# A hybrid decoder block on one core: VectorE instead of GpSimd at the passage, B's second value projection traced ahead of a norm, and the bonus of B's second segment traced later

## The chip, the cores and the metric

The kernel runs on one NeuronCore of a Trainium2 chip. The metric is device time in microseconds (us) of one execution; the kernel before has a median of 2935.78 us over 3 runs (2934.64 to 2939.5 us). The engines are called as the profile calls them: PE is TensorE (matrix products), PEld its loading of weights, DVE is VectorE, ACT is ScalarE, POOL is GpSimd, SP is SyncE, which issues most of the DMAs.

## The reference

One decoder layer over 1024 tokens and 16 meta tokens ahead of them, 1024 channels wide, in float32:

```
h = h + 0.5 * swiglu(rmsnorm(h), ffn1_w_gu, ffn1_w_down)
u = rmsnorm(h, mix_norm)
aq, ak, av, az, abeta, aalpha, bcols, ga, gb = split(u @ w_in)
o_a = deltanet(aq, ak, av, az, abeta, aalpha, ...)   # 8 heads, chunks of 64
o_b = rwkv7(bcols, ...)                              # 16 heads of 64
h = h + (sigmoid(ga) * o_a + sigmoid(gb) * o_b) @ w_out
h = h + 0.5 * swiglu(rmsnorm(h), ffn2_w_gu, ffn2_w_down)
out = rmsnorm(h, final_norm)[:, 16:]
```

Inside the RWKV-7 branch (B in the code) three projections r, k and v of `u` are shifted (each token is mixed with the token before it), a state is carried through the sequence, and a bonus is added to its output:

```
zf = zf + (prev - zf) * mu            # the shift
r, k, v, wd, ad, gd = split(zf)
k = k * (1 + (a - 1) * k_a)
y = scan(state, r, decay, k, v, -kk, kk * a);  y = groupnorm(y)
y = y + sum(r * k * r_k, over a head) * v     # the bonus
```

The DeltaNet branch (A) runs short causal convolutions over its q, k and v, normalises q and k, and inverts a unit lower triangular matrix for every chunk of 64 tokens.

## The kernel before, in words

**Precision.** A product of float32 matrices is made as three products of rounded parts: every operand is held as a high part and a low part (`split`, lines 162 and 163: ACT writes the high part, another engine subtracts it from the source and writes the low part), and `mm3` adds high*high, high*low and low*high. So one projection tile of 128 output channels is 8 x 3 = 24 products over the 8 blocks of 128 input channels (the name `pp` in the profile, line 314).

**Stages.** The first feed-forward layer (`down` and its forms are the tail of it, products `pd`, line 741) runs to about 691 us. Then comes the *passage*: the mix norm turns the residual `h` into the operand `u`. The tokens are in two segments of 512 (the first with the 16 meta tokens, 528 columns). The norm of the first segment is made there: ACT squares the blocks (`nsq`, line 327), an adder sums them (line 334), PE adds over partitions (`nps`), DVE multiplies each block `h` by gain and 1/rms (`nt`, line 918), and `u_tile` splits the result (`uk`, lines 162 and 163). For the other segment only the sums of squares are made here; the norm itself is made later. In the kernel before, POOL adds those sums (7 adds) and makes three of the eight low parts `uk` (blocks 1, 3 and 5). Then the middle: 16 steps, 8 for each segment, each of which handles 128 channels of A and of B; then the output projection; then the second feed-forward layer from about 2260 us to the end.

**A step.** The middle is a list of actions traced in the order of the strings `FIRST`, `REGULAR` and so on; a `+` stands for the next step. `new_b` makes B's projections v (48), k (40) and r (32), each by `shifted`: PE projects, ACT and DVE (lines 1205 and 1206) shift. It ends with the bonus: `bv = r*rk*k` on DVE (line 1485), split into `hl` (lines 162 and 163), two products `bon` with a block of ones (line 1292) and a multiplication by v on DVE (line 1490). `new_a` makes A's k, q and v with their convolutions (`acc`, line 1513) and column sums for the norms (`cs`, line 1292). `inverses` runs a long chain of small DVE instructions (`tb`, `Xb`, lines 1703 and 1705), copies the result (`Yt`, line 1706) and sends it through memory to `Xc`; `merge_blocks` (products `iv`, lines 1743 to 1767) joins the inverted blocks on PE with copies by ACT and DVE between: `Y` (line 1757), `XA` (line 1758), `T`. `operands` makes the products `grb` and `gra` and their masks (`LT`, line 1554). `norm` is the first action that deals with the segment that comes second.

**What sets the order.** Instructions are written by the trace, and a list scheduler of the framework then sets each engine's order from the order of tracing and its own estimate of when operands are ready; every engine takes its queue strictly in that order. `tc.issue_after` pins an instruction behind another. The number of buffers of a pool bounds how far ahead the scheduler can put work: projections write to PSUM tiles `mm` (two in the first segment, three in the second), column sums and the bonus to tiles `mx` (two, then three), and the parts `hl` have a single buffer, so that each user of `hl` waits for the products of the one before it.

Of the kernel before, what the change touches and what calls it, by code (L numbers as in the profile page):

```python
# [25 lines left out]
FULL = 512  # L26
# [131 lines left out]
def split(g, src, hi, lo, eng=None, hi_eng=None):  # L158
    if hi_eng:
        hi_eng.tensor_copy(hi, src)  # L160
    else:
        g.nc.scalar.activation(hi, src, AF.Copy)  # L162
    (eng or g.nc.vector).tensor_tensor(lo, src, hi.bitcast(F32), op=ALU.subtract)  # L163


LORA = (56, 57, 58)
USES = {"segment": LORA, "new_b": (48, 40, 32), "new_a": (8, 0, 16), "gates": (24, 59, 67)}


def schedule():  # L170
# [12 lines left out]

FIRST = "decay new_b tokens new_a decay+ operands norm inverses new_b+ new_a+"
REGULAR = "merge_blocks transitions operands+ inverses+ chains gates finish decay++ new_b++ finish_a new_a++"
BEFORE_SWITCH = "merge_blocks transitions operands+ inverses+ chains gates finish finish_a banks gates+ segment decay++ new_b++ tokens++ new_a++"
SWITCH = "merge_blocks transitions operands+ inverses+ chains finish decay++ new_b++ finish_a new_a++"
LAST_BUT_ONE = "merge_blocks transitions operands+ inverses+ chains gates finish finish_a"  # L190
FINAL = "gates merge_blocks transitions chains finish finish_a fill"

# [115 lines left out]
def mm3(g, ps, w, kk, rhs):  # L308
    n = 3 * kk
    i = 0  # L310
    for k in range(kk):
        hi, lo = rhs(k)
        for l, r in ((w[:, 0, k, :], hi), (w[:, 0, k, :], lo), (w[:, 1, k, :], hi)):
            g.last_product = g.nc.tensor.matmul(ps, lhsT=l, rhs=r, start=i == 0, stop=i == n - 1)  # L314
            i += 1


# [497 lines left out]
def ffn1(g):  # L815
    tc, nc = g.tc, g.nc
    n = T // 2
    with ExitStack() as ctx:
# [54 lines left out]
        def before_last():  # L873
# [5 lines left out]
            for x in ("t3", "22"):  # L879
# [9 lines left out]
            hidden.load(len(hidden.slots), LAST)  # L889
            logs(g)  # L890
            hooks.rms = [Rms(g, lambda: g.un.tile([P, 528], F32, name="nsq", tag="nsq", bufs=4), n,
                             add_on=nc.gpsimd if s else None) for s, (_, n, _) in enumerate(SEGS)]
            hooks.todo = []
            for s in range(2):
                for k in range(HK, KD):
# [2 lines left out]
        def squares(s, k):  # L898
            t0, sn, _ = SEGS[s]
            hooks.rms[s].add(hs[k][:, t0 : t0 + sn])  # L900
            nc.sync.dma_start(g.hdr[s][k], hs[k][:, t0 : t0 + sn])

        def after(r, m, s):
            if r < LAST:
                if r == LAST - 1 and m == HK - 1:
                    before_last()
                return
            squares(s, m)
            if m == HK - 1 and s == 0:
                rs = g.un.tile([P, 528], F32, name="nrs", tag="nrs", bufs=1)  # L910
                hooks.rms[s].finish(rs)
                g.u = []
                hooks.todo = [(k, rs) for k in range(KD)]
            elif m == HK - 1:
                nc.gpsimd.dma_start(g.rdr, hooks.rms[s].acc[:, :FULL])
            for k, rs in hooks.todo[: 2 * s]:
                t = hooks.nt[:, k]
                nc.vector.scalar_tensor_tensor(t, hs[k][:, SEGS[0][0] :], g.V("gm", k), rs, op0=ALU.mult, op1=ALU.mult)
                g.u.append(u_tile(g, t, nc.gpsimd if k in (1, 3, 5) else None))
            del hooks.todo[: 2 * s]  # L920

        hooks.after = after
        down(g, hs, 1, n, hidden, hooks)
# [208 lines left out]
def ch3(ap, c):  # L1132
    return ap.rearrange("p (a b) -> p a b", b=c)
# [161 lines left out]
def parts_tile(g, n):  # L1295

    t = g.st.tile([P, 2, 528], F32R, name="hl", tag="hl")
    return t[:, 0, :n], t[:, 1, :n]
# [137 lines left out]
    return q  # L1436


def new_b(g, q):

    nc, st, V, c, j, n, off, it = g.nc, g.st, g.V, q.c, q.j, q.n, q.off, q.it
# [2 lines left out]
    tmp = lambda name, w=528: tmp_tile(g, name, w)  # L1444
    EN, ELx, av, elm = q.EN, q.ELx, q.av, meta and q.elm

    v = shifted(g, c, 48 + j, 16 + j, "vB")


    Vs = q.Vs = st.tile([P, NCB, CB], F32, name="Vs", tag="Vs", bufs=2)  # L1450
# [32 lines left out]
    nc.vector.tensor_tensor(AR[:, NCB + 1 :], ch3(r[:, fs], CB), ELx[:, :, 1:], op=ALU.mult)  # L1483
    bv = q.bv = st.tile([P, FULL], F32, name="bv", tag="bv", bufs=2)
    nc.vector.scalar_tensor_tensor(bv, r[:, fs], V("rk", j), k[:, fs], op0=ALU.mult, op1=ALU.mult)
    ps = g.mx.tile([P, 512], F32, name="bon", tag="mx")
    hi, lo = parts_tile(g, FULL)
    split(g, bv, hi, lo)
    colsum(g, ps, "bd", hi, lo)
    nc.vector.tensor_tensor(bv, ps, v[:, fs], op=ALU.mult)  # L1490


def new_a(g, q):
# [233 lines left out]
def merge_blocks(g, q):  # L1727
# [28 lines left out]
    nc.scalar.activation(Y[0:32, :, 32:64], ch3(ps2[0:32, 0:384], 32), AF.Copy)
    nc.vector.tensor_copy(Y[64:96, :, 96:128], ch3(ps2[64:96, 0:384], 32))
    nc.vector.tensor_copy(XA[32:64, :, 0, :, :], ps2[32:64, 0 : NCA * 32].rearrange("p (t c r) -> p t r c", r=2, c=16))
# [215 lines left out]
def finish_a(g, q):  # L1974
# [11 lines left out]
    else:  # L1986
        g.last = yb


ACTIONS = {"new_b": new_b, "tokens": tokens, "new_a": new_a, "norm": norm, "operands": operands, "inverses": inverses, "merge_blocks": merge_blocks, "transitions": transitions,  # L1990
           "chains": chains,
           "gates": gates, "finish": finish, "finish_a": finish_a, "fill": fill}

# [85 lines left out]
```

## Time and profile before

| what | value |
|---|---|
| median of 3 runs | 2935.78 us (2934.64 to 2939.5) |
| the profiled execution, its own time | 2937.92 us |
| its span, first to last instruction | 2935.9 us |
| its mean granted PE clock | 0.993 |
| PE busy, of the span | 2829.0 us (96%) |
| DVE busy | 2198.7 us (75%) |
| ACT busy | 1445.4 us (49%) |
| POOL busy | 386.7 us (13%) |

PE is the engine with next to no room: all that the kernel can win without fewer products lies in the some 107 us in which PE is not busy, and in what the clock takes from it. So the profile is read by the places at which PE stands still: what released it there, and what the engine that released it had been doing. An entry such as `[1.09 <-ACT hl L162]` in a timeline says that PE had been idle for 1.09 us when an ACT instruction of line 162, which writes `hl`, let it go on.

### The profile page before, as it was taken

To read this page: it belongs to the slowest core of one execution; us is meant where nothing else is said; L and a number is where in the kernel's file an instruction comes from. 1 tells how busy PE (TensorE), PEld (TensorE's weight loads), DVE (VectorE), ACT (ScalarE), POOL (GpSimd) and SP (SyncE) were. 2 spreads that over 40 slices of the span, in tenths; PEclk is the share of its full clock that TensorE was granted. 3 is DMA by queue.
4 is the path that set the end of the run, shared out by engine and by line. 5 is a ranking of instruction groups with operands and counts; after the bars stand their busy time and mean duration, and the time that the engine had idled before them with its cause. 6 is when DMAs were issued, how large, how long until landed. Compare 5 with 4: busy or idle time off the path is not lost. (4 is left out here: it accounts for less than half of the span.)

```text
span 2935.9 us, 60624 instructions
## 1 busy us (share of the span) xinstructions
PE 2829.0 (96%) x24552; PEld 2447.1 (83%) x24552; DVE 2198.7 (75%) x4183; ACT 1445.4 (49%) x2511; POOL 386.7 (13%) x566
## 2 busy tenths in 40 slices
PE   8999999999899999999998999999999999999998
PEld 8999999999878887888776777777777888888887
DVE  8666567776678877788777888888877766667876
ACT  6322224346555656566566656656644422223443
POOL 0332320003000000000000110101101032232000
PEclk9999999999999999999999999999999999999999
DMA  5333226553232322333232332333355333223763
GB/s 215 127 109 103 101 99 226 189 193 126 67 78 73 88 65 76 78 82 94 82 99 67 94 77 73 80 87 85 112 142 184 129 108 104 101 95 129 259 213 112
DMA packets 287895, 339.16 MB, mean 116 GB/s; under 512 B 172704, under 2 KB 181024, under 8 KB 287616
## 3 DMA queue, kind: packets, MB, share of 16 engines
q1 hardware_dynamic: 283600, 326.10, 35.7%
q0 software_dynamic: 2000, 6.56, 0.6%
q8 instruction: 193, 3.16, 0.4%
q10 hardware_dynamic: 2016, 2.63, 0.3%
q14 instruction: 86, 0.70, 0.1%
HBM read 267.57 MB, written 73.41 MB: 116 GB/s over the span
## 5 line engine op out<-in xcount | busy, mean ns | idle before, releaser
L314 PE MATMUL pp<-uk,w 128*128 128x512 f32 (+2 forms) x4824 | 972.6, 347 | 7.4 <-ACT w L162 2.2
L314 PEld LDWEIGHTS pp<-uk,w 128*128 128x128 f32 x4824 | 745.3, 191 | 101.3 <-issue 5.6
L741 PE MATMUL pd<-form,w 128*128 128x256 f32 (+2 forms) x2904 | 435.1, 312 | 0.0
L741 PEld LDWEIGHTS pd<-form,w 128*128 128x128 f32 x2904 | 402.5, 189 | 32.3 <-issue 1.0
L520 PE MATMUL pg<-bt,w 128*128 128x256 f32 (+2 forms) x2520 | 401.6, 317 | 2.3 <-DVE w L163 2.3
L520 PEld LDWEIGHTS pg<-bt,w 128*128 128x128 f32 x2520 | 360.2, 188 | 36.3 <-DVE w L163 3.6
L526 DVE TENSOR_TENSOR c<-c,pg 128x520 f32<-128x520 f32 (+1 forms) x280 | 189.4, 688 | 247.4 <-PE pg L520 222.2
L163 DVE TENSOR_TENSOR w<-wraw,w 128x1024 fp32r<-128x1024 f32 (+1 forms) x254 | 334.1, 1316 | 41.9 <-ACT w L162 38.6
L520 PE MATMUL pg<-b,w 128*128 128x256 f32 (+2 forms) x2160 | 348.1, 317 | 1.1 <-DVE w L163 1.1
L162 ACT ACTIVATE w<-wraw 128x1024 fp32r<-128x1024 f32 (+1 forms) x254 | 267.0, 1052 | 161.1 <-PE pg L520 117.3
L520 PEld LDWEIGHTS pg<-b,w 128*128 128x128 f32 x2160 | 309.9, 188 | 29.4 <-DVE w L163 1.3
L162 ACT ACTIVATE w<-wrx 128x1024 fp32r<-128x1024 f32 (+1 forms) x64 | 58.4, 912 | 274.7 <-PE pg L520 246.2
L162 ACT ACTIVATE w<-wsum 128x768 fp32r<-128x768 f32 x96 | 75.7, 789 | 142.0 <-PE pd L741 116.7
L162 ACT ACTIVATE form<-form 128x520 fp32r<-128x520 f32 (+1 forms) x152 | 94.2, 632 | 83.6 <-DMA form<-frm 79.7
L1705 DVE TENSOR_TENSOR Xb<-Xb,tb 115x126 f32<-115x126 f32 (+22 forms) x496 | 125.6, 253 | 10.6
L490 POOL TENSOR_TENSOR wrx<-wrx 128x512 f32<-128x512 f32 x38 | 52.4, 1380 | 613.5 <-DVE w22b L163 440.6
L1703 DVE TENSOR_TENSOR tb<-Ub,Xb 115x126 f32<-115x126 f32 (+22 forms) x496 | 124.6, 251 | 9.1
L163 DVE TENSOR_TENSOR w<-wsum,w 128x768 fp32r<-128x768 f32 x96 | 87.2, 908 | 37.3 <-ACT w L162 37.2
L163 DVE TENSOR_TENSOR form<-form 128x520 fp32r<-128x520 f32 (+1 forms) x152 | 100.9, 697 | 17.6 <-ACT form L162 17.3
L1513 DVE SCALAR_TENSOR_TENSOR acc<-xr,pk,acc 128x528 f32<-128x528 f32 (+1 forms) x144 | 107.3, 756 | 5.9 <-ACT acc L1509 4.7
L314 PE MATMUL pwo<-uk,w 128*128 128x512 f32 x384 | 94.9, 397 | 2.1 <-DVE ho L1180 1.5
L314 PEld LDWEIGHTS pwo<-uk,w 128*128 128x128 f32 x384 | 70.2, 188 | 17.6 <-ACT w L162 2.8
(445 smaller groups left out, 4259.4 us busy)
## 6 DMA issues: line engine op xcount, KB each, us to landing
wraw<-in_win SPq DMA_DIRECT2D x150, 512.0 KB
wraw<-in_wgu SPq DMA_DIRECT2D x44, 512.0 KB
wrx<-in_wgu SPq DMA_DIRECT2D x44, 512.0 KB
frm<-c SPq DMA_DIRECT2D x76, 260.0 KB
form<-frm SPq DMA_DIRECT2D x76, 260.0 KB
frm<-c SPq DMA_DIRECT2D x76, 256.0 KB
form<-frm SPq DMA_DIRECT2D x76, 256.0 KB
wraw<-in_wdn SPq DMA_DIRECT2D x34, 384.0 KB
```

The source lines that it names most:

```text
L162: g.nc.scalar.activation(hi, src, AF.Copy)
L163: (eng or g.nc.vector).tensor_tensor(lo, src, hi.bitcast(F32), op=ALU.subtract)
L314: g.last_product = g.nc.tensor.matmul(ps, lhsT=l, rhs=r, start=i == 0, stop=i == n - 1)
L490: sums.tensor_tensor(a22, a21, a22, op=ALU.add)
L520: nc.tensor.matmul(ps[:, c0 : c0 + cn], lhsT=l[:, x, k, :], rhs=r[:, k, y, c0 : c0 + cn], start=i == 0, stop=i == 3 * HK - 1)
L526: nc.vector.tensor_tensor(o, x, y, op=ALU.add)
L741: nc.tensor.matmul(pd[:, c0 : c0 + cn], lhsT=wd[:, u, k - k0, :], rhs=x[:, v, c0 : c0 + cn], start=k + i == 0, stop=k == HF - 1 and i == 2)
L1513: nc.vector.scalar_tensor_tensor(acc[:, :n], xr[:, tap : tap + n], V("convw", ct * 4 + tap), acc[:, :n], op0=ALU.mult, op1=ALU.add)
L1703: nc.vector.tensor_tensor(tv, U[:, i, i + 1 :].unsqueeze(2).to_broadcast([npt, nt, ncc]), X[:, i, 0:ncc].unsqueeze(1).to_broadcast([npt, n ...
L1705: nc.vector.tensor_tensor(X[:, i + 1 :, 0:ncc], X[:, i + 1 :, 0:ncc], tv, op=ALU.add)
```

## The change

Four edits. (1) At the passage the adder of the second segment's sums and the low parts of blocks 1, 3 and 5 are DVE's instead of POOL's; for that segment the two norm multiplications and their splits are traced ahead of the square and add of the block just finished, where they stood behind them. The DMA `rdr` that stores the sums stays on POOL's queue. (2) `new_b` is cut: its value projection becomes an action of its own, `values_b`, traced right before `new_b` everywhere but in the opening, where the second step's `values_b` is traced ahead of `norm`. (3) The end of `new_b` becomes a function `bonus`; for the first segment it is called where it stood (with its PSUM tile taken after the split), for the second segment it is called in `new_a` after the second projection there, its products pinned behind the twelfth product of that projection. (4) In `merge_blocks` the copy `XA` is traced before the copy `Y` on DVE.

```
@@ schedule
-USES = {"segment": LORA, "new_b": (48, 40, 32), "new_a": (8, 0, 16), ...}
+USES = {"segment": LORA, "values_b": (48,), "new_b": (40, 32), "new_a": (8, 0, 16), ...}
-FIRST = "decay new_b tokens new_a decay+ operands norm inverses new_b+ new_a+"
-REGULAR = "... decay++ new_b++ finish_a new_a++"
+FIRST = "decay values_b new_b tokens new_a decay+ operands values_b+ norm inverses new_b+ new_a+"
+REGULAR = "... decay++ values_b++ new_b++ finish_a new_a++"
@@ mm3
+    g.products = []
...
+            g.products.append(g.last_product)
@@ the passage
-                             add_on=nc.gpsimd if s else None) for s, (_, n, _) in enumerate(SEGS)]
+                             add_on=None) for s, (_, n, _) in enumerate(SEGS)]
-            squares(s, m)
+            if not s:
+                squares(s, m)
...
-            elif m == HK - 1:
-                nc.gpsimd.dma_start(g.rdr, hooks.rms[s].acc[:, :FULL])
             for k, rs in hooks.todo[: 2 * s]:
...
-                g.u.append(u_tile(g, t, nc.gpsimd if k in (1, 3, 5) else None))
+                g.u.append(u_tile(g, t))
             del hooks.todo[: 2 * s]
+            if s:
+                squares(s, m)
+                if m == HK - 1:
+                    nc.gpsimd.dma_start(g.rdr, hooks.rms[s].acc[:, :FULL])
@@ new_b, bonus, new_a
+def values_b(g, q):
+    q.v_all = shifted(g, q.c, 48 + q.j, 16 + q.j, "vB")
...
-    v = shifted(g, c, 48 + j, 16 + j, "vB")
+    v = q.v_all
...
+    q.v = v[:, fs]
+    if meta:
+        bonus(g, q)
+def bonus(g, q, behind=None):
+    hi, lo = parts_tile(g, FULL)
+    split(g, q.bv, hi, lo)
     ps = g.mx.tile([P, 512], F32, name="bon", tag="mx")
-    hi, lo = parts_tile(g, FULL)
-    split(g, bv, hi, lo)
-    colsum(g, ps, "bd", hi, lo)
-    nc.vector.tensor_tensor(bv, ps, v[:, fs], op=ALU.mult)
+    with ExitStack() as queue:
+        if behind is not None:
+            queue.enter_context(g.tc.issue_after(behind.ins))
+        colsum(g, ps, "bd", hi, lo)
+    g.nc.vector.tensor_tensor(q.bv, ps, q.v, op=ALU.mult)
...
         ps = proj(g, c, ct)
+        if wi == 1 and not meta:
+            bonus(g, q, g.products[3 * HK - 1])
@@ merge_blocks
+    nc.vector.tensor_copy(XA[32:64, :, 0, :, :], ps2[32:64, 0 : NCA * 32].rearrange(...))
     nc.vector.tensor_copy(Y[64:96, :, 96:128], ch3(ps2[64:96, 0:384], 32))
-    nc.vector.tensor_copy(XA[32:64, :, 0, :, :], ps2[32:64, 0 : NCA * 32].rearrange(...))
```

How the order moves is read at three places. The first is DVE's queue at the passage, from the third of the last four blocks `h` on. Before:

```order
L918 SCALAR_TENSOR_TENSOR nt<-h_5076,pk,nrs 128x528
L918 SCALAR_TENSOR_TENSOR nt<-h_5074,pk,nrs 128x528
L918 SCALAR_TENSOR_TENSOR nt<-h_5081,pk,nrs 128x528
L163 TENSOR_TENSOR uk<-nt,uk 128x528 [waits Activation_49]
L918 SCALAR_TENSOR_TENSOR nt<-h_5078,pk,nrs 128x528
L163 TENSOR_TENSOR uk<-nt,uk 128x528 [waits Activation_49]
L748 SCALAR_TENSOR_TENSOR h_5076<-pd,h_5076 128x256 [waits PE_49]
L918 SCALAR_TENSOR_TENSOR nt<-h_5077,pk,nrs 128x528
L918 SCALAR_TENSOR_TENSOR nt<-h_5075,pk,nrs 128x528
L163 TENSOR_TENSOR uk<-nt,uk 128x528 [waits Activation_49] x2
L748 SCALAR_TENSOR_TENSOR h_5074<-pd,h_5074 128x256 [waits PE_49]
```

and with the change (line numbers are one or two higher there):

```order
L163 TENSOR_TENSOR uk<-nt,uk 128x528 [waits Activation_49] x2
L750 SCALAR_TENSOR_TENSOR h_5076<-pd,h_5076 128x256 [waits PE_49]
L919 SCALAR_TENSOR_TENSOR nt<-h_5081,pk,nrs 128x528
L919 SCALAR_TENSOR_TENSOR nt<-h_5078,pk,nrs 128x528
L336 TENSOR_TENSOR nsq<-nsq 128x512 [waits Activation_49]
L163 TENSOR_TENSOR uk<-nt,uk 128x528 [waits Activation_49] x2
L750 SCALAR_TENSOR_TENSOR h_5074<-pd,h_5074 128x256 [waits PE_49]
L919 SCALAR_TENSOR_TENSOR nt<-h_5077,pk,nrs 128x528
L919 SCALAR_TENSOR_TENSOR nt<-h_5075,pk,nrs 128x528
L336 TENSOR_TENSOR nsq<-nsq 128x512 [waits Activation_49]
L163 TENSOR_TENSOR uk<-nt,uk 128x528 [waits Activation_49] x2
```

All eight low parts and the adds are in DVE's queue now, in groups of one block `h`, two norms, one add and two low parts; the last two norms and low parts stand behind the last block of `h`, which waits for PE's last `pd` product.

The second place is PE's queue in the opening, where the first step's operands of A are made (`gm`, `bkt`, `vp`, `btp`, `ktp`, `vmp`) up to the first product `vbp` of the second step, which needs the shifted value projection `vB`. Before:

```order
L1600 MATMUL gm<-c3m,ck 16x16 [waits DVE_49,PE_49]
L1609 MATMUL gm_8579<-kq 16x16 [waits DVE_49,PE_49]
L1388 MATMUL bkt<-ck,BK 128x64 [waits DVE_49]
...
L1356 MATMUL vp<-LT,Vs 64x64 [waits Activation_49]
L1356 MATMUL vp<-LT,Vs 64x64 x15
L1356 MATMUL vp<-Vs,BKt 64x64 x5
L1641 MATMUL btp<-ck,bkm 64x128 [waits Activation_49]
L1646 MATMUL ktp<-ck,kq 128x128 [waits Activation_49]
L1646 MATMUL ktp<-ck,kq 128x128 x3
L1651 MATMUL vmp<-ck,kq 128x128 [waits Activation_49]
L351 MATMUL nps<-usq,ones 128x512 [waits DMAHW4_49,Activation_49]
L1356 MATMUL vbp<-ck,vB 64x64 [waits DVE_49]
```

and with the change:

```order
L315 MATMUL pp<-uk,w 128x272 x7
L1622 MATMUL gm<-c3m,ck 16x16 [waits DVE_49,PE_49]
L315 MATMUL pp<-uk,w 128x272 x8
L1631 MATMUL gm_8579<-kq 16x16 [waits DVE_49,PE_49]
L315 MATMUL pp<-uk,w 128x272 x7
L1393 MATMUL bkt<-ck,BK 128x64 [waits DVE_49]
...
L315 MATMUL pp<-uk,w 128x256 x9
...
L315 MATMUL pp<-uk,w 128x256 x6
L1361 MATMUL vp<-LT,Vs 64x64 [waits Activation_49]
L1361 MATMUL vp<-LT,Vs 64x64 x15
```

Between the waiting small products stand 47 products of the second step's r projection, in pieces; four stood there before. Its PSUM tile is free earlier because DVE's shift of `vB` is now ahead of the masks of `gra`.

The third place is PE's queue in a step of the second segment, from the products of q on (24 `pp` each make one projection). Before:

```order
L314 MATMUL pp<-uk,w 128x512 x24
L314 MATMUL pp<-uk,w 128x512 [waits Activation_49]
L314 MATMUL pp<-uk,w 128x512
L314 MATMUL pp<-uk,w 128x512 [waits DVE_49]
L314 MATMUL pp<-uk,w 128x512 x10
L1292 MATMUL bon<-hl,bdr 128x512 [waits PE_49,Activation_49]
L314 MATMUL pp<-uk,w 128x512 x7
```

and with the change, in the same step:

```order
L1297 MATMUL cs<-hl,onesr 128x512 [waits PE_49,Activation_49]
L1361 MATMUL vp<-Vs,BKt 64x64
L315 MATMUL pp<-uk,w 128x512 x2
L1297 MATMUL cs<-hl,onesr 128x512 [waits DVE_49]
L315 MATMUL pp<-uk,w 128x512 x8
L1297 MATMUL bon<-hl,bdr 128x512 [waits PE_49,Activation_49]
L315 MATMUL pp<-uk,w 128x512 x2
L1297 MATMUL bon<-hl,bdr 128x512 [waits DVE_49]
```

The two products `bon` stand behind A's k with its column sums instead of behind the first half of k's projection: some 80 products of 512 columns after the column sum of `kkn`, where it was 37.

More of the change, by code (lines that the diff above doesn't have):

```diff
@@ L166 @@
 LORA = (56, 57, 58)
-USES = {"segment": LORA, "new_b": (48, 40, 32), "new_a": (8, 0, 16), "gates": (24, 59, 67)}
+USES = {"segment": LORA, "values_b": (48,), "new_b": (40, 32), "new_a": (8, 0, 16), "gates": (24, 59, 67)}
 def schedule():
@@ L182, in schedule @@
                 yield act.rstrip("+"), it + act.count("+")
-FIRST = "decay new_b tokens new_a decay+ operands norm inverses new_b+ new_a+"
-REGULAR = "merge_blocks transitions operands+ inverses+ chains gates finish decay++ new_b++ finish_a new_a++"
-BEFORE_SWITCH = "merge_blocks transitions operands+ inverses+ chains gates finish finish_a banks gates+ segment decay++ new_b++ tokens++ new_a++"
-SWITCH = "merge_blocks transitions operands+ inverses+ chains finish decay++ new_b++ finish_a new_a++"
+FIRST = "decay values_b new_b tokens new_a decay+ operands values_b+ norm inverses new_b+ new_a+"
+REGULAR = "merge_blocks transitions operands+ inverses+ chains gates finish decay++ values_b++ new_b++ finish_a new_a++"
+BEFORE_SWITCH = "merge_blocks transitions operands+ inverses+ chains gates finish finish_a banks gates+ segment decay++ values_b++ new_b++ tokens++ new_a++"
+SWITCH = "merge_blocks transitions operands+ inverses+ chains finish decay++ values_b++ new_b++ finish_a new_a++"
 LAST_BUT_ONE = "merge_blocks transitions operands+ inverses+ chains gates finish finish_a"
@@ L1756, in merge_blocks @@
     nc.scalar.activation(Y[0:32, :, 32:64], ch3(ps2[0:32, 0:384], 32), AF.Copy)
+    nc.vector.tensor_copy(XA[32:64, :, 0, :, :], ps2[32:64, 0 : NCA * 32].rearrange("p (t c r) -> p t r c", r=2, c=16))
     nc.vector.tensor_copy(Y[64:96, :, 96:128], ch3(ps2[64:96, 0:384], 32))
-    nc.vector.tensor_copy(XA[32:64, :, 0, :, :], ps2[32:64, 0 : NCA * 32].rearrange("p (t c r) -> p t r c", r=2, c=16))
     ps3 = g.ch.tile([P, 512], F32, name="iv3", tag="ch")
@@ L1987, in finish_a @@
         g.last = yb
-ACTIONS = {"new_b": new_b, "tokens": tokens, "new_a": new_a, "norm": norm, "operands": operands, "inverses": inverses, "merge_blocks": merge_blocks, "transitions": transitions,
+ACTIONS = {"values_b": values_b, "new_b": new_b, "tokens": tokens, "new_a": new_a, "norm": norm, "operands": operands, "inverses": inverses, "merge_blocks": merge_blocks, "transitions": transitions,
            "chains": chains,
```

## Prediction

> **What bounds the kernel now.** I read the page first, for the engine without room.
>
> ```profile
> span 2935.9 us, 60624 instructions
> PE 2829.0 (96%) x24552; PEld 2447.1 (83%) x24552; DVE 2198.7 (75%) x4183; ACT 1445.4 (49%) x2511; POOL 386.7 (13%) x566
> ```
>
> PE is busy 96% of the span and the change adds no product, so a gain can only come out of the 2935.9 - 2829.0 = 107 us in which PE stands still, or out of products that run slower than they might. Next, the stretches that the change touches, side by side (busy time of each engine, then the granted PE clock).
>
> ```profile
> core 0: us, PE busy (x) PEld busy (x) DVE busy (x) ACT busy (x) POOL busy (x), PEclk, DMA share, GB/s
> 660.00:700.00 40.00, 37.23 (x287) 35.93 (x286) 30.76 (x36) 21.00 (x33) 16.92 (x12) 0.96 0.44 156
> 772.00:796.00 24.00, 17.73 (x253) 12.90 (x252) 13.79 (x37) 14.48 (x35) 1.55 (x7) 0.86 0.27 76
> 796.00:850.00 54.00, 49.19 (x382) 43.39 (x383) 42.78 (x106) 30.13 (x52) 6.83 (x16) 0.91 0.28 69
> 1600.00:2160.00 560.00, 533.38 (x5860) 416.05 (x5861) 464.15 (x1092) 339.25 (x639) 52.69 (x113) 1.00 0.32 86
> ```
>
> The passage (660 to 700) has 2.8 us of PE idle time, the opening (772 to 796) 6.3, the second segment (1600 to 2160) 26.6 in 560, that is some 4 in each step of 85 us. The opening and the passage also have a clock below 1. Stretches of 3.41 us show where it falls:
>
> ```profile
> 693.72:697.13 3.41, 1.25 (x5) 0.83 (x6) 3.32 (x4) 1.48 (x3) 3.14 (x3) 1.00 0.16 62
> 697.13:700.54 3.41, 3.40 (x16) 3.07 (x15) 0.88 (x3) 0.63 (x1) 1.81 (x2) 0.50 0.34 115
> 1577.77:1581.18 3.41, 1.11 (x4) 0.30 (x2) 3.41 (x9) 3.36 (x6) 3.21 (x6) 1.00 0.00 0
> 1581.18:1591.42 10.24, 8.34 (x45) 5.38 (x46) 9.65 (x24) 5.29 (x11) 0.43 (x1) 0.50 0.16 53
> 1840.60:1844.01 3.41, 2.81 (x12) 2.24 (x13) 3.41 (x5) 0.95 (x2) 3.03 (x4) 1.00 0.89 201
> ```
>
> In each pair a stretch in which PE was busy for 1.1 to 1.3 us of 3.41 is followed by one at half clock; 2.81 us of work (the stretch with the bonus' wait) is not punished. So a wait at the passage, in the opening or at the switch of segments costs its length and, where PE then has work, up to 1.7 us more for each half-clock stretch.
>
> **The passage.** DVE's queue and PE's waits there:
>
> ```profile
> 689.26 1.83 DVE L163 TENSOR_TENSOR uk<-nt,uk 128x528 fp32r<-128x528 f32 x1
> 691.01 0.76 DVE L918 SCALAR_TENSOR_TENSOR nt<-h,pk,nrs 128x528 f32<-128x528 f32 x1
> 691.69 0.69 DVE L163 TENSOR_TENSOR uk<-nt,uk 128x528 fp32r<-128x528 f32 x1
> 692.52 1.31 POOL L163 TENSOR_TENSOR uk<-nt,uk 128x528 fp32r<-128x528 f32 x1 [2.01 <-ACT uk L162]
> 692.64 3.46 DVE L918 SCALAR_TENSOR_TENSOR nt<-h,pk,nrs 128x528 f32<-128x528 f32 x2
> 693.89 0.51 PE L314 MATMUL pp<-uk,w 128*128 128x272 f32 x2 [0.62 <-POOL uk L163]
> 696.03 1.49 DVE L163 TENSOR_TENSOR uk<-nt,uk 128x528 fp32r<-128x528 f32 x2
> 696.78 5.49 PE L314 MATMUL pp<-uk,w 128*128 128x272 f32 x29 [1.26 <-DVE uk L163]
> ```
>
> PE waits for the operand blocks one by one, 0.62 us for POOL and 1.26 for DVE among it, and in the stretch 693.72 to 697.13 it stands still for 3.41 - 1.25 = 2.2 us; the last low part ends at 696.03 + 1.49 = 697.52. DVE is slow beside POOL: a low part 1.83 for 0.69, a norm 1.73 for 0.76. In the change DVE has, from the first of the four last blocks on, everything in its queue:
>
> ```profile
> 680.16 0.42 DVE L748 SCALAR_TENSOR_TENSOR h<-pd,h 128x256 f32<-128x256 f32 x1
> 675.60 0.71 DVE L334 TENSOR_TENSOR nsq<-nsq 128x528 f32<-128x528 f32 x1 [0.77 <-ACT nsq L327]
> 679.02 1.23 DVE L163 TENSOR_TENSOR w<-wraw,w 128x1024 fp32r<-128x1024 f32 x1 [2.72 <-ACT w L162]
> ```
>
> 4 blocks x 0.42 + 8 norms x 0.76 + 4 adds x 0.71 + 8 low parts x 0.69 + one weight 1.23 = 17.4 us in 25 instructions; neighbours overlap by some 0.08 (691.01 + 0.76 against 691.69), 2.0 in all, so 680.16 + 15.4 = 695.5, and about 0.3 for ACT's high parts: 695.8. That is **-1.7** against 697.52. Bounds: -2.8 (all the idle time of 660 to 700) and 0, if the last two norms, which now stand behind the last block `h`, are held up there: what queues behind that wait is two norms, an add, two low parts, and PE waits for these. PE's idle time then falls from 2.2 us in one stretch to about 1.5 over two, so the half-clock stretch at 697.13 may go: -1.7 at even odds, **-0.8**.
>
> **The opening.** PE's small products wait for DVE and ACT in turn; the last wait is for `vB`, and DVE's chain of the inverse starts behind it and ends in `Xc`, for which the first `iv` waits:
>
> ```profile
> 792.45 0.77 DVE L1206 SCALAR_TENSOR_TENSOR vB<-pp,pk,vB 128x528 f32<-128x528 f32 x1 [1.31 <-ACT vB L1205]
> 793.27 1.14 PE L1356 MATMUL vbp<-ck,vB 64*64 64x64 f32 x32 [2.24 <-DVE vB L1206]
> 835.50 0.91 SPq L1708 DMA_DIRECT2D scX<-Xb  x1
> 836.34 0.68 DVE L1947 TENSOR_TENSOR zg<-pp,zg 128x512 f32<-128x512 f32 x1
> 836.94 1.21 DVE L163 TENSOR_TENSOR w<-wraw,w 128x1024 fp32r<-128x1024 f32 x1
> 842.55 1.28 DVE L1554 TENSOR_TENSOR LT<-grb,ck 128x512 f32<-128x512 f32 x2
> 846.35 0.74 PE L1743 MATMUL iv<-Xc,LT 32*32 32x32 f32 x32 [1.81 <-DMA Xc<-scX]
> ```
>
> The 47 products of r now lie in these waits: at half of a 512-column product (24 in 5.74 us, the last row quoted below) 47 x 0.12 = 5.6 us of the 6.3. That is work moved forward, and it is worth something only if PE reaches what follows sooner. There the inverse decides: with the change DVE does, between its first `tb` and the copy `Yt`, four masks `LT` (2.6), three more `E`, `zg` (0.7), a weight (1.2) and another `acc` that came behind the copy before, less one shift: 5.1 us; it can start at most the wait before `vB` sooner (1.3). On SP's queue the stores `scX` of the inverse now come behind one more fetch of weights and two stores of `LT`; one of these is likely still being issued when the copy ends, 0.9 by the row of `scX`. So `Xc` lands 5.1 - 1.3 + 0.9 = 4.7 us later, with 6 us more of PE's work done by then (34 `pp` of 512 columns that came behind that `iv`, 34 x 0.24 = 8.1, less some 2 for `grb` and `xp` that go behind it): **-1.3**. Bounds: -6.3 (the waits go and the chain loses nothing) and +4.7 (the work moved forward is not missed later). Half-clock stretches ahead of `iv` don't count, since `Xc` and not PE sets that moment. On SP's queue the weights keep their order; only the norm's own loads come later, and what is queued behind them is not waited for here.
>
> **The second segment.** Here the waits repeat in every step:
>
> ```profile
> PE bon L1292 <- ACT hl L162: 6.3, 6, 1.2
> PE iv L1762 <- DVE XA L1758: 4.7, 7, 0.7
> PE mp L1356 <- ACT at L1834: 1.9, 7, 0.6
> PE np L1356 <- DVE AR L1844: 1.7, 7, 0.2
> 1840.52 0.63 ACT L162 ACTIVATE hl<-bv 128x512 fp32r<-128x512 f32 x1 [0.41 <-DVE bv L1485]
> 1841.20 0.51 PE L1292 MATMUL bon<-hl,bdr 128*128 128x512 f32 x1 [1.09 <-ACT hl L162]
> 1864.63 0.56 DVE L1757 COPY Y<-iv 32x384 f32<-32x384 f32 x1 [2.64 <-ACT Y L1756]
> 1865.20 0.28 DVE L1758 COPY XA<-iv 32x128 f32<-32x128 f32 x1
> ```
>
> The bonus moved behind 45 further products has its `hl` long before, so its 6.3 us in six steps go; `XA` ahead of `Y` is ready 0.56 sooner, of the 0.7 that `iv` waits: 0.56 x 7 = 3.9 us. `Y` comes 0.28 later, under the products `iv` of line 1762 and the ACT copy `T` that stand between it and its reader. Together 10.2. Not all of it stays. DVE is busy 464 of 560 us (83%) and its work is the same; a PE that is ahead by 1 us meets the next thing that DVE or ACT makes, the low parts of A's k and of its norms above all, which now come before the bonus. And the order leaves less filler between the first `iv` and `mp`. I take back 0.4 us a step in six steps, 2.4: **-7.8**. Bounds: -13 (the other waits shrink too) and +3 (all comes back and the thinner head costs 0.4 a step).
>
> The first segment's steps keep the bonus and only swap `XA` and `Y`; PE doesn't wait for `XA` there: 0. At the **switch** the bonus' wait goes too:
>
> ```profile
> 1581.43 0.79 PE L1292 MATMUL bon<-hl,bdr 128*128 128x512 f32 x1 [1.01 <-ACT hl L162]
> ```
>
> -1.0, and with some luck the three half-clock stretches from 1581.18, 5.1 us of lost clock; these hang on the stretch before them, whose idle 2.3 us (3.41 - 1.11) hold only some 0.8 of the bonus' wait, so three chances in ten: -1.5. **-2.5**, bounds -6 and +3. The work added to DVE before the passage's end (three adds at 663 to 669) and what follows on POOL's queue (`rdr`, stores) are waited for by nobody before the second segment: 0.
>
> **Sum.** -1.7 - 0.8 - 1.3 - 7.8 - 2.5 = -14.1. The profiled execution took 2937.92, 2.1 over the median but inside the runs shown (2934.64 to 2939.5); against it 2923.8, and by the median 2921.7. I take **2923 us**.
>
> The Trainium skill (TensorE: Matmul & The Clock Gate, part 1 on the HAM clock gate) says that the clock is watched in free-running windows of about 3.4 us, is halved after at least one idle window and restored after a busy one. The trace agrees in the length (697.13 to 700.54) but not in the word idle: a window with 1.25 us of work was enough. By the page's letter none of these places would be halved and the two clock terms would be 0: -11.8, and 2926.1 by the profiled execution.
>
> **Rivals.** (A) *The waits come back*: DVE, whose work is unchanged, paces the second segment, and PE waits for `hl` of A instead of the bonus. For it: DVE's 83%, and the 0.41 us that ACT waited for `bv`, which shows the chain and not the place as the cause. Against it: in 26.6 us of PE idle time only the named waits are large. Then only the passage, part of the opening and 1 us of the switch are left, some -4: 2934. (B) *The whole gain*: the named waits and the clock losses go: -1.7 - 1.7 - 6.3 - 10.2 - 6.1 = -26: 2912. Against it: `Xc`. (C) *Slower*: one mechanism, the head of a step of the second segment, from the first `iv` to `np`. Its links are a chain over PE, ACT and DVE; the change takes about four projection products (0.24 each, from the row below) and 20 small `grb` (0.02 to 0.03 each, as the 32 `iv` in 0.74) from between the links, 1.0 + 0.5 = 1.5 us a step. If the links can't close up, that becomes waiting: 7 x 1.5 = +10.5, and on top of rival A, whose -4 stays, +6.5: 2944. It decides once `mp` and `np` wait over 1 us more each step than now (0.27 and 0.24). Speaking against: the filler isn't gone, it stands where waits are. (D) *It doesn't do what it says*: the last two norms, behind the last `h`, end no sooner than now and the passage gains nothing. That takes 2.5 (1.7 + 0.8) from the sum, inside the forecast's range.
>
> ```profile
> 1825.49 5.74 PE L314 MATMUL pp<-uk,w 128*128 128x512 f32 x24
> ```
>
> **Chances.** The forecast with its bounds, 2915 to 2930, 0.50 (D within it); A, 2930 to 2939, 0.24; B, below 2915, 0.15; C, 0.11. What a measurement of this kernel can tell from no change is about 0.2%, 5.9 us: faster means below 2929.9, slower above 2941.7. The forecast is faster but for 0.04, B wholly: 0.61; with a part of A that ends a little lower 0.65; slower is C less a little, 0.09; the same 0.26. The range that leaves out 2 in 10 runs from 2909 to 2938: it takes in most of B and A and leaves out C.
>
> **What would show it.** In the changed profile: at the passage no POOL instruction of line 163 and norms of 0.76 each; the last low part near 695.8 and a clock of 1 behind it. In the opening no wait of 2.24 for `vB`, and `Xc` the thing that `iv` waits for, longer than 1.81. In the second segment `bon` not in the list of waits, `iv` waiting 0.1 for `XA`, a step of 84.3 us instead of 85.4. I am wrong if the steps stay at 85.4 with waits for `hl` (A), if `mp` and `np` lead the list (C), or if the opening gains more than `Xc` lets it.

## The result

The changed kernel takes 2919.83 us (median of 4 runs, 2918.24 to 2920.93), the kernel before beside it 2937.64 (4 runs, 2934.64 to 2940.07). The ratio is 0.9934, 95% interval 0.9922 to 0.9945: 17.8 us less between the medians, 16 to 23 by the interval. Forecast were 2923 and some 14 us. A second series gave 0.9937 (0.9925 to 0.995).

First the page of the changed kernel, for the engines.

```profile
span 2918.1 us, 60636 instructions
PE 2827.4 (97%) x24552; PEld 2448.4 (84%) x24552; DVE 2191.5 (75%) x4193; ACT 1447.0 (50%) x2511; POOL 387.4 (13%) x556
```

The products are the same in number; PE stands still for 2918.1 - 2827.4 = 90.7 us where it was 106.9. The other 1.6 us are busy time: the same products run faster, since fewer of them run at half clock. The same stretches as before, moved by what was won ahead of them:

```profile
660.00:700.00 40.00, 39.19 (x315) 38.24 (x314) 28.79 (x46) 22.28 (x35) 5.69 (x9) 1.00 0.48 161
768.00:792.00 24.00, 22.49 (x282) 18.30 (x280) 13.97 (x34) 14.41 (x33) 1.68 (x8) 1.00 0.27 76
792.00:846.00 54.00, 46.89 (x385) 39.15 (x383) 42.79 (x112) 31.70 (x57) 5.58 (x15) 0.97 0.29 71
1600.00:2150.00 550.00, 533.80 (x5687) 419.39 (x5684) 458.76 (x1100) 336.31 (x630) 64.30 (x106) 1.00 0.31 85
```

PE's idle time went from 2.8 to 0.8 us in the passage, from 6.3 to 1.5 in the opening, and from 26.6 to 16.2 in the second segment; behind the opening it rose, from 4.8 to 7.1. The clock is 1.00 in the first two, where it was 0.96 and 0.86.

To see where the time went I took, for a number of moments of the old trace, the share of PE's products (by columns) done by then, and asked when the new trace had done the same. New minus old, in us:

| by the old time | 690 | 705 | 780 | 990 | 1560 | 1610 | 1755 | 2140 | end |
|---|---|---|---|---|---|---|---|---|---|
| difference | -0.1 | -3.9 | -4.2 | -11.2 | -14.3 | -15.9 | -12.3 | -19.7 | -17.6 |

So the passage brought 3.8 us, the opening about 7, and the second segment wins, loses 3.6 in the step after the switch, and then wins 7.4. Two of these figures are soft. In a second execution of the same kernel the opening brings some 5 by this measure, because its clock was halved at other places too (from 806.38 and from 925.84 on). And at 1610, where the new order has other products in front, the difference is 14 to 18 by other weights of a product.

**The passage** on DVE, from the first of the four last blocks `h` on, and PE's two remaining waits:

```profile
679.90 0.42 DVE L750 SCALAR_TENSOR_TENSOR h<-pd,h 128x256 f32<-128x256 f32 x1
680.24 1.44 DVE L919 SCALAR_TENSOR_TENSOR nt<-h,pk,nrs 128x528 f32<-128x528 f32 x2
...
691.95 1.45 DVE L919 SCALAR_TENSOR_TENSOR nt<-h,pk,nrs 128x528 f32<-128x528 f32 x2
693.31 0.69 DVE L336 TENSOR_TENSOR nsq<-nsq 128x512 f32<-128x512 f32 x1
693.91 1.33 DVE L163 TENSOR_TENSOR uk<-nt,uk 128x528 fp32r<-128x528 f32 x2
693.45 0.64 PE L315 MATMUL pp<-uk,w 128*128 128x272 f32 x3 [0.20 <-ACT uk L162]
694.68 5.52 PE L315 MATMUL pp<-uk,w 128*128 128x272 f32 x43 [0.58 <-DVE uk L163]
```

Two norms take 1.45 us where they took 3.46 beside POOL. The last low part ends at 695.24 instead of 697.52, and no half-clock stretch follows: from 694.68 on 43 products take 5.52 us where 29 took 5.49. All four traces with the old passage have such a stretch, which starts between 695.5 and 697.5; none of the nine with the new passage has it.

**The opening.** The list of PE's waits between 770 and 796 has three entries left:

```profile
PE grb L1573 <- DVE LT L1576: 0.7, 1, 0.7
PE vbm L1467 <- ACT Vs L1464: 0.5, 1, 0.5
PE gra L1612 <- DVE LT L1576: 0.3, 1, 0.3
```

The wait of 2.24 us for `vB` is gone, and so are the small ones for `gm`, `bkt`, `vp` and `nps`. Then the chain of the inverse and what it ends in:

```profile
790.33 0.77 DVE L1211 SCALAR_TENSOR_TENSOR rB<-pp,pk,rB 128x528 f32<-128x528 f32 x1 [0.87 <-ACT rB L1210]
791.01 0.18 DVE L1725 TENSOR_TENSOR tb<-Ub,Xb 115x31 f32<-115x31 f32 x1
831.59 0.60 DVE L1728 COPY Yt<-Xb 115x512 f32<-115x512 f32 x1
842.88 0.75 PE L1765 MATMUL iv<-Xc,LT 32*32 32x32 f32 x32 [1.30 <-DMA Xc<-scX]
```

`Xc` lets the first `iv` go at 842.88: 3.5 us sooner than before, where the forecast had it 4.7 later. That is not the opening's doing: with the passage alone this `iv` starts at 842.12. What the opening did is taken up below.

**The second segment**, PE's waits from the switch on (1580 to 2150):

```profile
PE pp L315 <- DVE w L163: 5.1, 3, 3.0
PE np L1361 <- DVE AR L1866: 4.2, 6, 1.7
PE cs L1297 <- ACT hl L1311: 3.4, 7, 0.9
PE mp L1361 <- ACT at L1856: 2.4, 7, 0.6
PE cs L1297 <- DVE hl L1312: 1.8, 4, 0.5
PE iv L1784 <- DVE XA L1779: 0.9, 1, 0.9
```

`bon` is not in it and `iv` waits once for `XA` instead of seven times. New are three waits for the low parts of weights and a larger one for `AR`.

### The profile page after: what moved, and what is told of

Its sections match the earlier page's. It is cut to its first block, busy times and chain, and to the rows that moved or that the text cites. A ratio compares the mean times of both kernels' runs of the same rounds, so it can differ in the third digit from the quotient of the medians.

```text
span 2918.1 us, 60636 instructions
## 1 busy us (share of the span) xinstructions
PE 2827.4 (97%) x24552; PEld 2448.4 (84%) x24552; DVE 2191.5 (75%) x4193; ACT 1447.0 (50%) x2511; POOL 387.4 (13%) x556
## 4 chain that ended last, share of the span: by engine, by line
PE 74%; DVE 14%; ACT 7%; issue 3%; DMA 2%; SPq 0%; POOL 0%; DVEq 0%; ACTq 0%; POOLq 0%
PE pg L522 25%; PE pp L315 19%; PE pd L743 14%; DVE w L163 2%; PE pwo L315 2%; PE pg L546 2%; DVE tb L1725 2%; DVE Xb L1727 2%; ACT w L162 1%; PE cs L1297 1%; PE gra L1612 1%; DVE mt L1863 1%; PE vp L1361 1%; PE b L1938 1%; PE p L1913 1%
## 5 line engine op out<-in xcount | busy, mean ns | idle before, releaser
L1727 DVE TENSOR_TENSOR Xb<-Xb,tb 115x126 f32<-115x126 f32 (+22 forms) x496 | 126.1, 254 | 10.5
L163 DVE TENSOR_TENSOR form<-form 128x520 fp32r<-128x520 f32 (+1 forms) x152 | 101.2, 701 | 19.9 <-ACT form L162 19.7
```

Of the source, the lines that this page charges most:

```text
L1727: nc.vector.tensor_tensor(X[:, i + 1 :, 0:ncc], X[:, i + 1 :, 0:ncc], tv, op=ALU.add)
```

## The experiments

All times are device times; each kernel ran in five rounds (5 to 11 executions) beside the kernel before on the same chip. The four edits are the passage (1), the opening (2), the bonus (3) and the swap of `XA` and `Y` (4).

**Each edit alone.** The kernels are the one before with the hunks of one edit from the diff above; the first, for example, is

```
-                             add_on=nc.gpsimd if s else None) for s, (_, n, _) in enumerate(SEGS)]
+                             add_on=None) for s, (_, n, _) in enumerate(SEGS)]
...
-                g.u.append(u_tile(g, t, nc.gpsimd if k in (1, 3, 5) else None))
+                g.u.append(u_tile(g, t))
```

with the norms traced ahead of the add. Expected for it:

> The kernel before with edit 1 alone (sums, low parts and their order at the passage on VectorE). Theory, from the two traces laid side by side: the passage pays by itself, 1.8 us of waits and one half-clock stretch of 1.7 us, together -3.5, and nothing of it is given back later. First rival, the sum on record: -2.5 (the half-clock stretch only at even odds). Second rival: PE comes earlier into the opening, where VectorE's chain sets the pace, and waits there for what it won: 0.

For the second (`values_b` as an action, its second call ahead of `norm`, nothing else):

> The kernel before with edit 2 alone (the second step's value projection traced ahead of the norm). Theory, from the traces: the waits between 772 and 796 are filled and the inverse's chain starts so much earlier that Xc lands no later than before; -6 to -9 by 900 us, of which some 2 are given back in the first segment's steps: about -6. Rival, the step on record: Xc lands 4.7 us later because VectorE does 5.1 us more ahead of the copy Yt: -1.3.

For the third (`bonus` as a function, called in `new_a` for the second segment):

> The kernel before with edit 3 alone (bonus of the second segment behind twelve products of A's k). Theory: the steady steps win, about 1 us each in five steps, and the first three steps of the second segment lose most of it again to waits for the low parts of weights and for AR (2.95, 1.65 and 1.67 us in the changed trace): -2. Rival, the sum on record: -6.3 in six steps and -1 at the switch, less 2.4 of new waits: -5.

For the fourth (two lines of `merge_blocks` change places):

> The kernel before with edit 4 alone (XA copied ahead of Y). Theory: the wait of iv for XA goes from 0.70 to 0.14 us in seven steps, -3.9 in all, and shows in steps of 84.9 instead of 85.4 us. Rival: the next links of the head (xp, which waits for Y, and mp) wait for it instead, and the steps stay at 85.4: 0.

Measured, with the kernel before at 2939.6 us (24 runs):

| kernel | median us | ratio, 95% interval | us by the ratio |
|---|---|---|---|
| passage alone | 2935.83 | 0.9986 (0.9977 to 0.9995) | -4.1 (-6.8 to -1.5) |
| opening alone | 2930.67 | 0.9969 (0.9958 to 0.9981) | -9.1 (-12.3 to -5.6) |
| bonus alone | 2930.13 | 0.9966 (0.9956 to 0.9977) | -10.0 (-12.9 to -6.8) |
| swap alone | 2939.66 | 1.0 (0.9991 to 1.0009) | 0 (-2.6 to +2.6) |

The passage pays what the changed kernel's trace shows; the interval holds both -3.5 and the sum on record, -2.5, but not 0. In its own trace, of an execution of 2937.87 us, the passage alone is 5.2 us ahead at 740 and 1.3 at 990: behind the first `iv` PE runs at half clock for 13.65 us there, where it was 6.83 before. The opening's -1.3 on record lies outside its interval; that `Xc` lands no later, as expected here, was wrong too: it came 3.0 us later, and the gain came all the same. The bonus is worth about twice the -5 and far more than the -2 that I had read from the changed trace. The swap is worth nothing that this can tell. The singles add up to 23 us, the whole is 17 to 19: something is paid twice or taken back in company.

The distance between the first products `gat<-gds` (lines 1958 to 1983 of the kernels) of successive steps, in us, tells more than the totals. The last steps of the first segment and the steady steps of the second:

| kernel | first segment, steady | over the switch (two steps) | next | next | steady |
|---|---|---|---|---|---|
| before | 92.6 | 205.4 | 86.3 | 85.4 | 85.4 |
| swap alone | 92.3 | 205.2 | 85.7 | 85.0 | 85.1 |
| bonus alone | 92.6 | 202.1 | 86.5 | 83.4 | 83.5 |
| changed | 92.3 | 198.5 | 92.0 | 86.2 | 84.0 |

The bonus alone takes 2.0 us from a step, more than the 1.1 of its own wait; the swap alone takes 0.3 to 0.4; in the changed kernel, which has both, it is only 1.4, and two steps behind the switch are long (the step over the switch is 3.6 shorter than with the bonus alone). Why, the timeline between the links of `iv` shows. With the bonus alone, in a steady step:

```profile
1857.57 2.56 PE L315 MATMUL pp<-uk,w 128*128 128x512 f32 x10
1858.40 0.48 ACT L1770 ACTIVATE Y<-iv 32x384 f32<-32x384 f32 x1
1858.92 0.56 DVE L1771 COPY Y<-iv 32x384 f32<-32x384 f32 x1 [1.13 <-ACT Y L1770]
1859.50 0.69 DVE L1531 TENSOR_TENSOR acc<-acc,xr 128x512 f32<-128x512 f32 x1
1860.23 0.28 DVE L1772 COPY XA<-iv 32x128 f32<-32x128 f32 x1
1860.84 0.56 PE L1776 MATMUL iv<-XA,UA 64*64 64x64 f32 x5
```

`XA` is copied after `Y` and even after an `acc`, and `iv` doesn't wait for it: ten projection products lie before it, 2.56 us, where before the change 32 `grb` lay, 1.10 us. In the kernel before that same place was

```profile
1863.82 1.10 PE L1551 MATMUL grb<-AR,BK 64*64 64x128 f32 x32
1865.63 0.52 PE L1762 MATMUL iv<-XA,UA 64*64 64x64 f32 x5 [0.70 <-DVE XA L1758]
```

So the moved bonus shifts products into the head of the step and covers the wait for `XA` as well. The swap then has nothing left to remove, and it makes the scheduler put less there: six products, 1.65 us, in the changed kernel.

**The whole without one edit, and the swap in some steps only.** The changed kernel once more as the yardstick of its series:

> The changed kernel once more, beside the next three on the same chip. Every theory: -17 to -20 us against the kernel before.

The changed kernel with the two lines of `merge_blocks` back in their old order:

```
-    nc.vector.tensor_copy(XA[32:64, ...], ps2[32:64, ...])
     nc.vector.tensor_copy(Y[64:96, :, 96:128], ch3(ps2[64:96, 0:384], 32))
+    nc.vector.tensor_copy(XA[32:64, ...], ps2[32:64, ...])
```

> The changed kernel with edit 4 undone (Y copied ahead of XA again). Theory: the copies' order costs time once the bonus is moved; the steps of the second segment go from 84.0 back to 83.4 us as with the bonus alone, the two long steps after the switch (92.0 and 86.2) to 86.5 and 83.4, and the first segment's steps from 92.3 to 92.6: -8 - 2 + 2 = 8 us less than the changed kernel, -26 against the kernel before. Rival, the sum on record: XA's wait comes back with 0.56 us in seven steps, 4 us more than the changed kernel, -14.

The same with a condition, `XA` first where `q.s == 0` (the first segment):

```
+    if not (q.s == 0):
+        nc.vector.tensor_copy(Y[64:96, :, 96:128], ch3(ps2[64:96, 0:384], 32))
     nc.vector.tensor_copy(XA[32:64, ...], ps2[32:64, ...])
+    if q.s == 0:
         nc.vector.tensor_copy(Y[64:96, :, 96:128], ch3(ps2[64:96, 0:384], 32))
```

> The changed kernel with XA ahead of Y in the first segment's steps only. Theory: both gains, 92.3 us a step in the first segment and 83.4 in the second; 2 us less than without the swap, -28 against the kernel before. Rival: the copies' order matters little by itself and the difference of the second segment's steps comes from where the scheduler happens to put other work; then this order too can have long steps: -14 to -28.

The changed kernel with the bonus at the end of `new_b` in all steps:

> The changed kernel with edit 3 undone (bonus at the end of new_b in all steps). Theory: what is left is the passage, the opening and the swap, -4, -6 to -9 and 0: -11, and the second segment's steps are 85.0 us, the wait for the bonus at 1.1 in each. Rival: the parts overlap, and without the bonus' move the gain falls by all of the 10 us that it brought alone: -9.

And, in a later series, the condition `q.it < 7` instead of `q.s == 0`, which leaves out the step over the switch,

> The changed kernel with XA ahead of Y only in the first seven steps, Y first again from the switch of segments on. Theory: 92.3 us a step in the first segment, 83.3 in the second and no long step after the switch: 2 us less than without the swap (2917.1), about 2915 or -24 against the kernel before, and at least as fast as with the swap in all eight steps of the first segment (2915.5). Rival: the step lengths around the switch are accidents of the order, and it lies anywhere between 2914 and 2920.

and the changed kernel with `new_b` whole again:

> The changed kernel with edit 2 undone (the second step's value projection with the rest of new_b again). Theory: the opening is worth in company what it is worth alone, 6 to 9 us: 2926 to 2929. Rival, the sum on record: 1.3 us, 2921.5. A second rival: the parts overlap, since the three single edits add up to 23 us and the whole is 18 to 19; then the opening is worth some 4 us less in company, 3 to 5.

Measured (the kernel before 2938.57 us in the first four, 2938.54 in the last two):

| kernel | median us (lowest to highest) | ratio, 95% interval |
|---|---|---|
| changed | 2920.18 (2919.21 to 2920.61) | 0.9937 (0.9925 to 0.995) |
| changed, without the swap | 2917.13 (2913.6 to 2920.82) | 0.9928 (0.9916 to 0.9941) |
| changed, swap in the first segment | 2915.46 (2914.62 to 2917.1) | 0.9923 (0.991 to 0.9935) |
| changed, without the bonus' move | 2923.76 (2923.12 to 2924.28) | 0.995 (0.9936 to 0.9963) |
| changed, swap in seven steps | 2917.09 (2914.36 to 2919.25) | 0.9927 (0.9914 to 0.9939) |
| changed, without the opening | 2927.66 (2924.21 to 2930.57) | 0.9961 (0.9948 to 0.9975) |

Without the swap the steps are as the theory said, 86.6, 83.3 and then 83.3 us, but the step over the switch is 202.0 instead of 198.5, and a good part of the 8 us is gone: 3 us remain between the medians, with ranges that overlap. With the swap in the first segment only, the steady steps are 83.3 as well while the step over the switch is short and the next one long (197.7 and 92.4); it is 4.7 us faster than the changed kernel, and the two ranges don't touch. By the median it is the best version here, 22.6 us (19 to 26) less than the kernel before; the ranges without the swap and with the swap in seven steps overlap with its own. Leaving out the step over the switch gives 206.5 and 86.6 there. So the rival of the two conditional swaps has its point: what a step gains is stable, and the two or three steps around the switch come out differently with each order. The step over the switch varies by 8 us (198.5 to 206.5); the step behind it takes part of that back, and both together vary from 288.6 to 293.1.

In company the bonus is worth 3.6 us (2923.76 - 2920.18), not 10; without it the gain is 14.8, which both the theory (11) and its rival (9) missed. The changed kernel was not run with the old passage, so what the passage is worth in company is not shown. With the swap the bonus' move makes the long steps, and the wait for `XA` that it covers is already gone. The waits of these steps (1655 to 1740) in the changed kernel

```profile
PE pp L315 <- DVE w L163: 2.2, 2, 1.7
PE np L1361 <- DVE AR L1866: 1.7, 1, 1.7
PE cs L1297 <- ACT hl L1311: 0.9, 1, 0.9
```

and without the swap

```profile
PE np L1361 <- DVE AR L1866: 0.5, 1, 0.5
PE cs L1297 <- ACT hl L1311: 0.4, 1, 0.4
```

show what is late there: the low parts of a weight, which DVE makes behind other work. Why the scheduler puts that work ahead of them in these steps and not in later ones I did not find out.

The opening is worth 7.5 us in company (2927.66 against 2920.18, each beside a kernel before of 2938.5), and by the ranges 3.6 to 11.4, so the -1.3 on record falls here too; 3 to 5 us, the second rival, lies at the low end.

The pin of the bonus behind the twelfth product does nothing by itself: built without it, the program has the same instructions in the same order on every engine (it was not run). It is tracing the bonus in `new_a` that moves it.

**What sets the first `iv`.** To see whether the landing of `Xc` sets PE's moment there, the inverse of the first step was made longer by copies that change no value:

```
+    if q.it == 0:
+        for _ in range(8):
+            nc.vector.tensor_copy(X, X)
     nc.vector.tensor_copy(Yt, X.rearrange("p t c -> p c t"))
```

> The changed kernel with eight more VectorE copies of Xb onto itself at the end of the first step's inverse, ahead of the copy Yt (they change nothing in the values). Some 2 to 4 us of work by the copies' length in the trace. Theory (the landing of Xc sets the moment of the first iv, as the wait of 1.3 us there says): the whole kernel is longer by about that time, 2922 to 2924. Rival: PE finds other work or wins the time back in the next step, as it gave back 2 us of the opening's gain: no difference, 2920.

Measured: 2926.89 us (2926.4 to 2928.25), 0.9961 (0.9949 to 0.9974), 6.7 us over the changed kernel and more than the theory's 2922 to 2924. The trace:

```profile
831.31 3.66 DVE L1730 COPY Xb<-Xb 115x512 f32<-115x512 f32 x8
841.18 0.87 PE L1983 MATMUL gat<-gds,ug 128*128 128x512 f32 x3
841.89 0.40 PE L1983 MATMUL gat<-g,ug 128*128 128x512 f32 x1
842.12 2.77 PE L315 MATMUL pp<-uk,w 128*128 128x272 f32 x21
846.25 0.75 PE L1768 MATMUL iv<-Xc,LT 32*32 32x32 f32 x32 [1.36 <-DMA Xc<-scX]
870.72:874.13 3.41, 2.40 (x14) 1.96 (x14) 2.85 (x10) 3.10 (x8) 0.42 (x6) 1.00 0.10 13
874.13:884.37 10.24, 9.23 (x61) 7.57 (x60) 5.96 (x19) 6.22 (x16) 0.37 (x2) 0.50 0.13 48
```

3.66 us of copies move `iv` by 3.37 (842.88 to 846.25), so `Xc` does set that moment; in all 13 traces `iv` starts 11.1 to 11.8 us behind the start of `Yt`. But PE stands still for it no longer than in the changed kernel (1.36 us against 1.30): 25 products (`gat` and `pp`), which come behind the `iv` there, fill the delay. The price is paid 25 us later, where these products are missing: in a stretch with more waiting PE's work fell to 2.40 of 3.41 us, many of its products narrow, and three stretches at half clock followed, in which PE was busy 90% of the time. By the third step's `gat` the kernel is 6.1 us behind the changed one.

## Why the prediction was right, and where not

The direction and the size within the range were right, and so was the mechanism at the passage and at the bonus' wait. The account of the opening and the sum of bonus and swap were wrong. That the total came so close is in part luck: by the traces the opening brought some 5 us more than forecast, the second segment with the switch some 5 less.

- **Passage, -1.7 and -0.8 on record.** Measured -3.8 in the trace and -4.1 (-6.8 to -1.5) alone. The sum of DVE's queue gave 695.8 for the last low part; it was 695.24. The term for the clock, at even odds, came in full: the half-clock stretch at 697.13 is gone. The rival that the last two norms are held up behind the last block `h` did not happen: the block came at 691.62, right behind the low parts.
- **Opening, -1.3 on record: wrong.** By the runs it is -9.1 alone and -7.5 in company; by the traces, at the first `gat<-gds` of the third step, -5.5 and -6.3. The -1.3 was +4.7 for a later `Xc` less 6 for work that is done by then. The starts of the links, in us, show both parts; the last column is the time from the first `iv` to that `gat`:

| trace | first `tb` | `Yt` | first `iv` | `iv` to `gat` |
|---|---|---|---|---|
| before | 794.24 | 834.94 | 846.35 | 212.5 |
| opening alone | 795.89 | 838.12 | 849.37 | 204.0 |
| changed, without the opening | 788.85 | 829.65 | 840.83 | 212.2 |
| changed | 791.01 | 831.59 | 842.88 | 203.8 |
| changed, second execution | 791.07 | 833.15 | 844.44 | 204.4 |

  `Xc` does come later by the opening, as forecast, but by 3.0 us alone and 2.1 in company (3.6 in the second execution) instead of 4.7. All three parts of the 4.7 failed. The chain was to start 1.3 sooner; it starts 1.7 (2.2) later, since the shift of `rB` and its wait now stand ahead of the first `tb`. The stores were to cost 0.9; from `Yt` to `iv` nothing is added (11.4 and 11.3 alone, 11.2 and 11.3 in company). And 5.1 us of DVE work ahead of `Yt` were to make the chain that much longer; it is as long as before, or 1.5 longer. The two chains, from the first `tb` to `Yt`, before and after:

```profile
794.24:834.94 40.70, 38.23 (x249) 35.06 (x242) 36.06 (x101) 23.96 (x41) 4.81 (x10) 0.89 0.16 52
```

```profile
791.01:831.59 40.58, 34.77 (x289) 29.41 (x288) 39.92 (x112) 26.45 (x47) 3.24 (x10) 0.96 0.22 72
```

  DVE does 3.9 us more (39.92 against 36.06, eleven instructions) in the same time. Before, it had stood still inside the chain. The waits of DVE in that stretch were

```profile
DVE rB L1206 <- ACT rB L1205: 1.8, 1, 1.8
DVE kq L1521 <- ACT xr L1313: 1.4, 1, 1.4
DVE hl L1307 <- ACT hl L1306: 0.5, 1, 0.5
DVE kB L1206 <- ACT kB L1205: 0.3, 1, 0.3
```

  4.0 us in all. The new order has r's projection done before the chain begins, and its list has one wait of 0.9 for `rB`, ahead of the first `tb`. I had added the work to the chain and had not looked for the waits in it, though DVE's 42.8 busy us of 54 behind 796, quoted there, say that it stood still now and then.

  The wait for `xr` goes with the clock. With the opening alone, and in the second execution of the changed kernel, it is there and the chain takes 42.2 and 42.1 us. That second execution had

```profile
802.97:806.38 3.41, 2.02 (x35) 1.30 (x35) 3.41 (x9) 3.16 (x6) 0.27 (x1) 1.00 0.00 0
806.38:809.79 3.41, 3.41 (x16) 3.41 (x16) 3.41 (x9) 2.20 (x5) 0.00 (x0) 0.50 0.46 154
DVE kq L1543 <- ACT xr L1318: 1.3, 1, 1.3
```

  Eight of the 13 traces have this wait, each some 9 us behind the start of a stretch at half clock; the five others have neither. So half-clock stretches ahead of `iv`, which on record "don't count", can count: between these two executions of one kernel the chain is 1.5 us longer and the `iv` 1.6 later.

  The larger part lies behind the `iv`, where 6 us were counted: the time from there to the third step's `gat` is 8.5 us shorter alone and 8.4 in company. Behind the `iv` PE had run at half clock,

```profile
847.31:854.14 6.83, 6.83 (x34) 4.57 (x31) 1.47 (x3) 0.96 (x2) 0.76 (x3) 0.50 0.34 50
```

  busy all the time, and after the change it runs there at full clock (842.88 on). That is 3.4 us, a term that the forecast did not have; the other 5 fit the work moved forward, put at 6. The five traces with the old opening all have such a stretch 0.6 to 1.3 us behind that `iv`, 6.83 us long or, in two of them, 13.65 (and there it is 215.4 us to the `gat`); of the eight with the new opening none has it there.
- **Bonus and swap, -6.3 and -3.9 less 2.4 on record.** The -10.2 of both waits was counted as two gains; the runs show that the bonus' move alone removes both waits (-10.0) and the swap alone gives nothing that can be told (0, though 0.3 to 0.4 us a step in its trace). The error is in the sentence that the order leaves less filler between the first `iv` and `mp`: at the link that waited for `XA` it puts more there. What I took back, 2.4, was too little: in the changed kernel the steady steps are 84.0 and not 83.4, and two steps lose 8 against the bonus alone, of which the step over the switch brings back 3.6. From 1610 to 2140 the trace gives -3.8 in place of -7.8; with the switch it is -5.4 in place of -10.3. Rival C named waits that did grow, `np` and `mp`, but not the size: 4.2 and 2.4 us in all, 3.0 more than before and not 10.5. And the list of waits quoted with the forecast left out its second row,

```profile
PE cs L1292 <- ACT hl L1306: 5.1, 13, 1.5
```

  more than the 4.7 for `XA`. The four rows that it did quote are 14.6 of the 26.6 us, so it is not true that only these waits were large. The wait of `cs` for ACT is 3.4 us in the changed kernel.
- **First segment, 0 on record.** The swap takes 0.3 us from each of its steps.
- **Switch, -2.5 on record.** From 1560 to 1610 the trace gives -1.6 (by other weights of a product -0.6 to -3.7). The wait for the bonus is gone and one of 3.0 for a weight's low part is new (the longest in the list); 6.8 us at half clock instead of 10.2 remain.

## What to carry to other kernels

When work is moved ahead of a chain's end on its engine, look first for the idle time within the chain: added work costs only what doesn't fit there. Take the moment at which a chain ends from a kernel that differs by that one edit; in the whole, another edit can have moved it. Two edits that each remove a wait from the same stretch of a queue are not to be added before one has asked whether one of them already covers the other's, and an edit that pays nothing alone may cost something in company. Keep the stable gain of a loop's step apart from the steps at its ends, which an order search reshuffles each time.

## What the runs showed of the hardware

PE's clock is halved for stretches of 3.41 us after a stretch that had waits, and idle time alone doesn't decide it: 1.11, 1.25 and 1.60 us of busy time of 3.41 (the last at 843.90) were followed by half clock, and so was 2.40 us where the work was mostly 128 columns wide and narrower, while 2.81 us of 512-column products (at 1840.60) was not.

```profile
843.90:847.31 3.41, 1.60 (x62) 1.31 (x59) 0.00 (x0) 0.00 (x0) 0.56 (x2) 1.00 0.90 219
```

At 1.7 us for each stretch in which PE has work this doubles the price of a wait of 2 us, and it makes a delay cost more than itself: 3.7 us in the longer chain became 6.7. Whether narrow products count less was not measured by itself, and the limit is a band: in the 13 traces (without the first 15 us and the last windows of each) all 48 windows of 3.41 us at full clock with PE busy for up to 1.43 us were followed by half clock, none with more than 2.41 was, and in between both happened. One kernel can fall on either side: 2.02 us behind 802.97 was followed by half clock in the second execution of the changed kernel, 2.04 at the same place was not in the first. Nor does a busy window always end it: with the passage alone PE was busy through all of 13.65 us at half clock (842.82 on). The Trainium skill (TensorE: Matmul & The Clock Gate, part 1) has the clock halved after an idle window of some 3.4 us; none of the windows quoted here was idle, and the term that its letter would have struck from the passage came in full.
